# Scores of 64-wide heads: the queries' hi times the keys' lo on 128 rows, with a zero-padded block of queries, in place of 64 rows

## The chip, the cores and the metric

The kernel runs on one core of a Trainium2 chip. The metric is device time in microseconds (us), the median of three executions. One execution was also profiled; its trace is what the rows below come from. TensorE (PE) multiplies, VectorE (DVE) and ScalarE (ACT) work elementwise, GpSimd (POOL) does small elementwise work and issues some DMAs, and SyncE (SP) issues the weight loads. PEld is TensorE's loading of its stationary operand, which the profile lists beside the products.

## The reference

Two transformer blocks over 512 tokens of width 1024, in float32. Three places in them form scores between heads of width 64, and only these are touched by the change:

```
diff_attention:        sc = einsum('bqhcd,bkhcd->bchqk', q, k) * 64**-0.5      # 4 heads x 2, then softmax and a difference
chunk_band_attention:  sc = einsum('bqhd,bkhd->bhqk', q, k) * scale + bias     # 8 heads, softmax
dsa_attention:         s  = einsum('bqhd,bsd->bqhs', iq, ik) * idx_scale       # 16 index heads, one shared key
                       score = sum_h relu(s) * iw; sel = top_k(score, 128)
                       logits = q . k[sel] * 64**-0.5 + bias                   # 8 heads, softmax
```

Everything else (projections, up and down products, gates, a convolution, a recurrence) is large matrix products and elementwise work.

## The kernel before

Every operand of a product is split into two parts, hi and lo, whose sum is the float32 value; a product of two such operands is three products (hi·hi, hi·lo, lo·hi) that accumulate in one PSUM bank (`mm3`, lines 130 to 132, one "block" = three products of 128x512). Weights come as a stream of 512 KB loads, are split by ACT (L117) and DVE or POOL (L118), and feed generators of blocks.

For heads of 64 the kernel saves one of the three products. `pack_q` puts a head's 64 rows of hi and its 64 rows of lo above each other in one tile (`qhl`; for the odd head of a pair lo stands on top), `pack_k` makes a tile with the keys' hi twice (`khh`) and one with the lo of both heads of a pair (`kl`). `score` then makes two products into the same PSUM bank: L431, `qhl` against `khh` over all 128 rows (that is hi·hi + lo·hi), and L432, the head's own 64 rows of `qhl` against the same 64 rows of `kl` (hi·lo). The stationary operand is always 128 queries of one row tile i; the moving width is W = 128(i+1), since keys behind the row tile are not needed.

`score` is called in four stages. A: the first block's differential attention (tile `psa`, 4 heads x 4 row tiles = 16 steps of two scores, 32 in all), each score followed by a small bf16 product that masks a corner (L548, preceded by its own load of `identb`). B: the banded attention (`psc`, 16 steps, 32 scores, no mask product). I: the indexer (`psi`, 16 heads x row tiles 3, 2, 1 = 48 scores), where DVE sums the heads' relu (L899) and afterwards picks the 128 highest scores in 16 rounds per row tile (L908, L909); I call that stage S. D: the sparse attention (`psc` again, 32 scores, each followed by a bf16 mask product, L356).

A, B and D run as pipelines: a step is a generator, each `yield` is a round, and after each round the tracer puts some blocks of other products behind it (`self.fill(rate)`), which keep TensorE busy while DVE and ACT work on the softmax. The order of the instructions on each engine is fixed when the program is built. The bias tables of B and D (`bt`) are loaded by DMAs that POOL issues (L327), with a small memset on POOL behind each table in B (L329).

Of the kernel before, what the change touches and what calls it, by code (L numbers as in the profile page):

```python
# [8 lines left out]
F32 = mybir.dt.float32  # L9
F32R = mybir.dt.float32r  # L10
# [18 lines left out]
WBUFS = 2  # L29
RBUFS = 3  # L30
# [7 lines left out]
# the order of the banded attention's query (0) and key (1) tiles  # L38
# [25 lines left out]
def groups(n, head):  # L64
    """(first, length): a group of head, then ones"""
    return [(0, head)] + [(a, 1) for a in range(head, n)]


class Kern:
# [34 lines left out]
    def stream(self, src, eng=None):  # L104
        """yields (hi, lo) [128, 1024]: the next eight blocks; src [loads, 128, 1024]"""
# [21 lines left out]
    def mm3(self, out, w, x, start, stop):  # L127
        """w, x: (hi, lo) pairs; w stationary"""
        mm = self.nc.tensor.matmul
        mm(out, w[0], x[0], start=start, stop=False)  # L130
        mm(out, w[0], x[1], start=False, stop=False)  # L131
        return mm(out, w[1], x[0], start=False, stop=stop).ins  # L132

    # Products are generators: a step is one block. True: done a step; False: an operand
    # is not there yet.
    def fm(self, src, xs, evac, first=0, head=1, eng=None):
        """output tiles [128 features, tokens]: the first head tiles together, the contraction
        outermost, then one by one"""
# [16 lines left out]
    def tm512(self, src, xs, evac, eng=None):  # L155
        """token-major [tokens, 512 columns]: src [4, 128, 1024], rows of 512 over the contraction"""
# [21 lines left out]
    def lead(self, gen, n):  # L178
        """n blocks of gen; what the context traces for TensorE is queued behind them"""
# [4 lines left out]
    def fill(self, n):  # L184
        """traces up to n steps (a fraction carries over) of the products in line"""
# [12 lines left out]
    def finish(self, gen=None):  # L198
        """traces the line up to gen's end, or all of it"""
# [7 lines left out]
    def split(self, src, name, scale=None, n=T, tag="o", tag2=None):  # L207
        """(hi, lo) of src * scale, scale one value per partition"""
# [12 lines left out]
    def sumsq(self, xs, gain=None, n=T, sq_eng=None):  # L221
        """squares summed over the tiles"""
# [14 lines left out]
    def token_mean(self, acc, n=T, div=D, parts=P, eps=EPS):  # L237
        """summed over the partitions / div + eps, token-major [128, n/128]"""
# [10 lines left out]
    def norm(self, gen, acc):  # L249
        """1 / rms of the tokens, token-major and along the free axis, gen's first blocks between"""  # L250
# [11 lines left out]
    def diag(self, rs, n=T):  # L262
        """rs on the diagonals of [128, 128] blocks, as hi and lo"""
# [16 lines left out]
    def bcast(self, rs, n=T, dg=None):  # L280
        """[128, n] with rs[token] along the free axis on every partition"""
# [9 lines left out]
    def consts(self):  # L291
# [7 lines left out]
        self.corner = self.cp.tile([P, CUT], BF, name="corner")  # L299
        nc.sync.dma_start(self.vecs[:, :8], d["vecs"][:, :8])  # L300
# [5 lines left out]
        nc.vector.memset(self.corner[:CUT], NEG)  # L306

# [6 lines left out]
    def toeplitz(self, ext):  # L314
        """ext: two of [8, 384] -> loader of a head's table [128, 512]: row q is ext[255 - q:767 - q].
        Copies of ext one row apart in DRAM, read with a row step one short of a copy."""
# [17 lines left out]
    def bias_attention(self, qT, kT, v, load, masks, out, rate, packed=False):  # L334
        """qT, kT: 4 tiles of two heads, q scaled; v: token tiles [128, 512];
        masks: per query tile (mask [128, width] bf16, first column), or None when the
        table holds the mask; out: a list for 4 (hi, lo) feature tiles."""
# [3 lines left out]
        def step(p, i):  # L341
            W = P * (i + 1)
            if i == 0:
                st[p, "bt"] = [load(2 * p + a, masks is None) for a in range(2)]
            es, pts = [], []
            for a in range(2):
                h, r = 2 * p + a, slice(64 * a, 64 * a + 64)
                ps = self.ps.tile([P, T], F32, name="psc", tag="ps")
                if packed:
                    self.score(ps, qT[h], kT[h], 64 * a, i, W, masks is None)  # L350
# [40 lines left out]
    def pipeline(self, steps, rate, every=1):  # L391
        """traces the stages of successive steps, a step starting every so many rounds, and
        rate blocks of the products in line after each round"""
# [11 lines left out]
    # Scores of heads of 64 in float32 by two products: a head's (hi, lo) of the queries one above  # L405
    # the other against (hi, hi) of the keys, then hi against lo.
    def pack_q(self, z, tags):
        """z: two heads; -> a tile for each, hi in the head's rows and lo in the others"""
# [8 lines left out]
    def pack_k(self, z, tag):  # L417
        """z: two heads; -> for each (hi, hi), and the lo of both"""
# [9 lines left out]
    def score(self, ps, q, k, a, i, W, last=True):  # L428
        """ps: a row tile's scores of the head in rows a on of its tile"""
        w, r = q[:, i * P:i * P + P], slice(a, a + 64)  # L430
        self.nc.tensor.matmul(ps[:, :W], w, k[0][:, :W], start=True, stop=False)  # L431
        self.nc.tensor.matmul(ps[:, :W], w[r], k[1][r, :W], start=False, stop=last)  # L432

    def to_feature(self, o, name, scale=None, tag="y"):
        """four token blocks [128 tok, 4, 128 features] -> (hi, lo) feature tile"""
# [6 lines left out]
    def gelu2(self, u, t):  # L442
        """twice gelu of u (tanh form), into t"""
# [13 lines left out]
    def mix(self):  # L457
# [50 lines left out]
        # lambda  # L508
# [15 lines left out]
        # bias of the banded attention  # L524
# [13 lines left out]
        def step(h, i):  # L538
# [3 lines left out]
            r0 = st[h, "r0"]  # L542
            es, sm = [], self.small("sm2", 2)
            mx = self.small("mx2", 2)
            for c in range(2):
                ps = self.ps.tile([P, T], F32, name="psa", tag="ps")
                self.score(ps, qa[2 * h + c], ka[2 * h + c], 64 * c, i, W, False)
# [837 lines left out]
```

## Time and profile before

| what | value |
|---|---|
| median of three executions | 2321.76 us (2319.76 to 2322.29) |
| the profiled execution, span from first to last instruction | 2320.4 us; the page gives no other time for it |
| PE busy | 98% of the span |
| DVE busy | 60% |
| ACT busy | 39% |
| POOL busy | 10% |
| stage A | 94 to 187 us |
| stage B | 210 to 365 us |
| stage I | 989 to 1051 us |
| stage S | 1051 to 1131 us |
| stage D | 1119 to 1226 us |

The stages are read from the first and last instruction on their PSUM tiles. A busy PE is not a PE at its peak: the end of each product is modelled, so the length of a product on TensorE is read here from the start of one to the start of the next, and never from the listed duration.

### The profile page before, as it was taken

To read this page: it belongs to the slowest core of one execution; us is meant where nothing else is said; L and a number is where in the kernel's file an instruction comes from. 1 tells how busy PE (TensorE), PEld (TensorE's weight loads), DVE (VectorE), ACT (ScalarE), POOL (GpSimd) and SP (SyncE) were. 2 spreads that over 40 slices of the span, in tenths; PEclk is the share of its full clock that TensorE was granted. 3 is DMA by queue.
4 is the path that set the end of the run, shared out by engine and by line. 5 is a ranking of instruction groups with operands and counts; after the bars stand their busy time and mean duration, and the time that the engine had idled before them with its cause. 6 is when DMAs were issued, how large, how long until landed. Compare 5 with 4: busy or idle time off the path is not lost.

```text
span 2320.4 us, 28792 instructions
## 1 busy us (share of the span) xinstructions
PE 2268.6 (98%) x11254; PEld 1814.6 (78%) x11254; DVE 1391.8 (60%) x2391; ACT 914.8 (39%) x1426; POOL 235.6 (10%) x258
## 2 busy tenths in 40 slices
PE   7999999999999999998999999999999999999997
PEld 6777777888788888766667888888877778888886
DVE  7676555766443433579876777733465656777534
ACT  5454343544332222453463444422222234444322
POOL 3101100000111100113130000000111210000001
PEclk9999999999999999999999999999999999999999
DMA  4413323432533333322212333333321123333333
GB/s 141 98 55 92 91 64 100 146 91 73 101 97 100 95 97 100 94 61 78 73 46 86 96 95 97 100 95 99 91 64 56 56 64 91 100 95 97 100 93 107
DMA packets 62535, 207.27 MB, mean 89 GB/s; under 512 B 8216, under 2 KB 12384, under 8 KB 62400
## 3 DMA queue, kind: packets, MB, share of 16 engines
q1 hardware_dynamic: 58368, 198.60, 28.2%
q0 software_dynamic: 2880, 5.79, 1.7%
q8 instruction: 88, 1.44, 0.2%
q10 hardware_dynamic: 1152, 1.05, 0.1%
q14 instruction: 47, 0.39, 0.0%
HBM read 201.74 MB, written 3.67 MB: 89 GB/s over the span
## 4 chain that ended last, share of the span: by engine, by line
PE 91%; DVE 5%; ACT 1%; issue 1%; DMA 1%; POOL 1%; SPq 0%; DVEq 0%; ACTq 0%
PE pg L130 27%; PE pg L132 26%; PE pg L131 26%; PE pl L1112 1%; PE po L384 1%; PE ptr L372 1%; PE psc L432 1%; PE psi L432 1%; DVE wlo L118 1%; DVE isc L909 1%; PE psc L431 1%; DMA wraw<-in_w_in 1%; DVE m L908 1%; PE poh L1156 1%; PE poh L1155 0%
## 5 line engine op out<-in xcount | busy, mean ns | idle before, releaser
L117 ACT CAST whi<-wraw 128x1024 fp32r<-128x1024 f32 (+1 forms) x368 | 386.1, 1049 | 746.9 <-PE pg L131 472.3
L118 DVE TENSOR_TENSOR wlo<-wraw,whi 128x1024 fp32r<-128x1024 f32 (+1 forms) x356 | 436.4, 1226 | 314.6 <-ACT whi L117 308.9
L130 PE MATMUL pg<-fg2h,whi 128*128 128x512 f32 x704 | 274.1, 389 | 0.0
L132 PE MATMUL pg<-fg2h,wlo 128*128 128x512 f32 x704 | 273.9, 389 | 0.0
L131 PE MATMUL pg<-fg2l,whi 128*128 128x512 f32 x704 | 273.9, 389 | 0.0
L130 PEld LDWEIGHTS pg<-fg2h,whi 128*128 128x128 f32 x704 | 132.1, 188 | 27.6
L131 PEld LDWEIGHTS pg<-fg2l,whi 128*128 128x128 f32 x704 | 132.1, 188 | 27.5
L132 PEld LDWEIGHTS pg<-fg2h,wlo 128*128 128x128 f32 x704 | 132.1, 188 | 27.1
L132 PE MATMUL pg<-m2h,wlo 128*128 128x512 f32 (+1 forms) x374 | 140.9, 377 | 0.6 <-DVE wlo L118 0.6
L130 PE MATMUL pg<-m2h,whi 128*128 128x512 f32 (+1 forms) x374 | 141.0, 377 | 0.0
L131 PE MATMUL pg<-m2l,whi 128*128 128x512 f32 (+1 forms) x374 | 140.8, 377 | 0.0
L130 PE MATMUL pg<-fgh,whi 128*128 128x512 f32 x352 | 137.3, 390 | 0.9 <-ACT whi L117 0.9
L132 PE MATMUL pg<-fgh,wlo 128*128 128x512 f32 x352 | 137.1, 389 | 0.0
L131 PE MATMUL pg<-fgl,whi 128*128 128x512 f32 x352 | 137.0, 389 | 0.0
L1005 DVE SCALAR_TENSOR_TENSOR yc<-zc,vecs,yc 128x511 f32<-128x511 f32 (+1 forms) x176 | 130.8, 747 | 2.7
L130 PE MATMUL pg<-xgh,whi 128*128 128x512 f32 x256 | 105.3, 411 | 7.5 <-ACT xgh L216 6.4
L259 POOL TENSOR_TENSOR rs<-ms,mhalf 128x4 f32<-128x4 f32 (+1 forms) x11 | 12.9, 1175 | 945.3 <-DVE ms L246 591.4
L1001 DVE TENSOR_TENSOR zc<-pg,rsb 128x512 f32<-128x512 f32 x88 | 60.5, 688 | 74.1 <-PE pg L132 74.1
L131 PE MATMUL pg<-xgl,whi 128*128 128x512 f32 x256 | 101.7, 397 | 0.5 <-DVE xgl L217 0.5
L132 PE MATMUL pg<-xgh,wlo 128*128 128x512 f32 x256 | 102.0, 398 | 0.0
L132 PEld LDWEIGHTS pg<-m2h,wlo 128*128 128x128 f32 x374 | 70.4, 188 | 13.8 <-DVE wlo L118 0.8
L130 PEld LDWEIGHTS pg<-m2h,whi 128*128 128x128 f32 x374 | 70.3, 188 | 13.0
(422 smaller groups left out, 4790.1 us busy)
## 6 DMA issues: line engine op xcount, KB each, us to landing
wraw<-in_ffn_up SPq DMA_DIRECT2D x88, 512.0 KB, 3.5
wraw<-in_ffn_down SPq DMA_DIRECT2D x48, 512.0 KB, 3.5
wraw<-in_w_gate_up SPq DMA_DIRECT2D x44, 512.0 KB, 3.5
wraw<-in_w_in SPq DMA_DIRECT2D x39, 512.0 KB, 3.6
wraw<-in_c_in SPq DMA_DIRECT2D x32, 512.0 KB, 3.5
wraw<-in_ab SPq DMA_DIRECT2D x29, 512.0 KB, 3.6
wraw<-in_w_down SPq DMA_DIRECT2D x22, 512.0 KB, 3.6
wraw<-in_w_ckv SPq DMA_DIRECT2D x16, 512.0 KB, 3.6
```

Source lines behind the costliest of these rows:

```text
L117: nc.scalar.copy(hi[:, p], raw[:, p])
L118: eng.tensor_tensor(lo[:, p], raw[:, p], hi[:, p], op=ALU.subtract)
L130: mm(out, w[0], x[0], start=start, stop=False)
L131: mm(out, w[0], x[1], start=False, stop=False)
L132: return mm(out, w[1], x[0], start=False, stop=stop).ins
L372: nc.tensor.transpose(pt[:, j * P:j * P + P], es[a][:, j * P:j * P + P], self.ident)
L384: nc.tensor.matmul(po[r, i * P:i * P + P], v[j][:, c0:c0 + 64], pts[a][:, j * P:j * P + P], start=j == 0, stop=j == i)
L431: self.nc.tensor.matmul(ps[:, :W], w, k[0][:, :W], start=True, stop=False)
L432: self.nc.tensor.matmul(ps[:, :W], w[r], k[1][r, :W], start=False, stop=last)
L908: nc.vector.max(m8, a)
L1001: nc.vector.tensor_tensor(z, ps, rsb, op=ALU.mult)
L1005: nc.vector.scalar_tensor_tensor(y[:, sh:], z[:, :T - sh], self.col(f"cw{l}{j}", f), y[:, sh:], op0=ALU.mult, op1=ALU.add)
```

## The change

The second product of a score takes all 128 rows. In A, B and D a new helper `pad_q` copies the head's 64 rows of hi for the row tile into one of six tiles `zq` of 128x128 (three for heads whose hi stands on top, three for the others), whose other 64 rows were set to zero by six memsets on POOL at the start; the copy runs on POOL. The product is then `zq` against the whole `kl` tile. The copies of a step are issued in a round of their own, one `yield` ahead of its scores, so each pipeline is one round longer, and a copy waits until TensorE has read what stood in the tile three steps before. In I no copy is needed: both halves of the key's lo tile hold the same rows, and the second product takes `qhl` itself (so lo·lo is added as well). To make room for the six tiles, the scratch of POOL's DMA descriptors is halved to 8192 bytes per partition. The rest of the diff removes comments.

```diff
+ZBUFS = 3
...
+        self.zq, self.zn = [[self.cp.tile([P, P], F32R, name=f"zq{a}{n}") for n in range(ZBUFS)] for a in range(2)], 0
...
+        for z in self.zq[0] + self.zq[1]:
+            nc.gpsimd.memset(z.bitcast(F32), 0.0)
...
+            zs = [self.pad_q(qT[2 * p + a], 64 * a, i) for a in range(2)]
+            yield
...
-                    self.score(ps, qT[h], kT[h], 64 * a, i, W, masks is None)
+                    self.score(ps, qT[h], kT[h], zs[a], i, W, masks is None)
...
-    def score(self, ps, q, k, a, i, W, last=True):
-        w, r = q[:, i * P:i * P + P], slice(a, a + 64)
-        self.nc.tensor.matmul(ps[:, :W], w, k[0][:, :W], start=True, stop=False)
-        self.nc.tensor.matmul(ps[:, :W], w[r], k[1][r, :W], start=False, stop=last)
+    def pad_q(self, q, a, i):
+        z = self.zq[a // 64][self.zn % (2 * ZBUFS) // 2]
+        self.zn += 1
+        self.nc.gpsimd.tensor_copy(z[a:a + 64], q[a:a + 64, i * P:i * P + P])
+        return z
+    def score(self, ps, q, k, w, i, W, last=True):
+        q = q[:, i * P:i * P + P]
+        self.nc.tensor.matmul(ps[:, :W], q, k[0][:, :W], start=True, stop=False)
+        self.nc.tensor.matmul(ps[:, :W], q if w is None else w, k[1][:, :W], start=False, stop=last)
...
+            zs = [self.pad_q(qa[2 * h + c], 64 * c, i) for c in range(2)]
+            yield
...
-                self.score(ps, qa[2 * h + c], ka[2 * h + c], 64 * c, i, W, False)
+                self.score(ps, qa[2 * h + c], ka[2 * h + c], zs[c], i, W, False)
...
-            self.score(ps, iq[h], idx["k"], 64 * (h % 2), i, W)
+            self.score(ps, iq[h], idx["k"], None, i, W)
...
-    nc = _bacc.Bacc("TRN2", target_bir_lowering=False, num_devices=1)
+    nc = _bacc.Bacc("TRN2", target_bir_lowering=False, num_devices=1, dynamic_dma_scratch_size=8192)
```

On TensorE, the second step of stage A (row tile 1, W = 256), before and then after; `pta` are transposes, `pg` blocks of other products:

```order
L566 MATMUL pta<-ident,ea 128x128
L431 MATMUL psa<-khh,qhl 128x256
L432 MATMUL psa<-kl,qhl 128x256
L548 LDWEIGHTS identb
L548 MATMUL psa<-corner,identb 128x64
L431 MATMUL psa<-khh,qhl 128x256
L432 MATMUL psa<-kl,qhl 128x256
L548 LDWEIGHTS identb
L548 MATMUL psa<-corner,identb 128x64
```

```order
L582 MATMUL pta<-ident,ea 128x128
L445 MATMUL psa<-khh,qhl 128x256
L446 MATMUL psa<-kl,zq_100 128x256
L564 LDWEIGHTS identb
L564 MATMUL psa<-corner,identb 128x64
L445 MATMUL psa<-khh,qhl 128x256
L446 MATMUL psa<-kl,zq_103 128x256
L564 LDWEIGHTS identb
L564 MATMUL psa<-corner,identb 128x64
```

The products, their widths and their order are the same; the second one takes `zq`. In stage I not even a name changes.

On POOL, from the last head's norm of stage A (`rs`) into stage B, before and then after; `bt` are the bias tables, the L438 rows the new copies:

```order
L259 TENSOR_TENSOR rs<-hss,mhalf 128x4 x4
L327 DMA bt<-ext_dram 32x512 x5
L329 MEMSET bt 64x64
L327 DMA bt<-ext_dram 32x512 x7
L329 MEMSET bt 64x64 x2
L327 DMA bt<-ext_dram 32x512 x4
L329 MEMSET bt 64x64
L327 DMA bt<-ext_dram 32x512 x5
```

```order
L260 TENSOR_TENSOR rs<-hss,mhalf 128x4
L331 DMA bt<-ext_dram 32x512 x5
L333 MEMSET bt 64x64
L331 DMA bt<-ext_dram 32x512 x5
L333 MEMSET bt 64x64
L331 DMA bt<-ext_dram 32x512 x3
L333 MEMSET bt 64x64
L331 DMA bt<-ext_dram 32x512 x2
L438 COPY zq_100<-qhl 64x128
L331 DMA bt<-ext_dram 32x512
L438 COPY zq_103<-qhl 64x128
L333 MEMSET bt 64x64
```

The two copies that the first step of B needs (`zq_100`, `zq_103`) stand behind 15 and 16 DMA issues and three memsets; before, no instruction of TensorE waited for POOL there.

On TensorE, the end of stage B, from the last step's scores (W = 512) on, before and then after; `pg<-ob` are blocks of the product that follows, `po` and `ptr` the rest of the attention:

```order
L431 MATMUL psc<-khh,qhl 128x512
L432 MATMUL psc<-kl,qhl 128x512
L431 MATMUL psc<-khh,qhl 128x512
L432 MATMUL psc<-kl,qhl 128x512
L130 MATMUL pg<-obh,whi 128x512
L131 MATMUL pg<-obl,whi 128x512
L132 MATMUL pg<-obh,wlo 128x512
```

```order
L445 MATMUL psc<-khh,qhl 128x512
L446 MATMUL psc<-kl,zq_100 128x512
L445 MATMUL psc<-khh,qhl 128x512
L378 MATMUL ptr<-ident,sc 128x128
L390 MATMUL po<-pT,vb 64x128
L378 MATMUL ptr<-ident,sc 128x128
L390 MATMUL po<-pT,vb 64x128
```

Before, four blocks (twelve products) followed the last scores; after, they stand ahead of them.

## Rows read from the trace of the kernel before

**Rows 1.** The page: busy us of each engine, share of the span, instructions.

```profile
PE 2268.6 (98%) x11254; PEld 1814.6 (78%) x11254; DVE 1391.8 (60%) x2391; ACT 914.8 (39%) x1426; POOL 235.6 (10%) x258
```

**Rows 2.** Windows A, B, I, S, D: length, busy us of PE, PEld, DVE, ACT, POOL, clock, DMA.

```profile
94.00:200.00 106.00, 105.58 (x527) 82.64 (x526) 75.75 (x188) 53.79 (x121) 3.56 (x3) 1.00 0.21 65
200.00:365.00 165.00, 162.72 (x816) 122.65 (x816) 84.27 (x215) 67.28 (x139) 18.11 (x41) 1.00 0.28 84
...
989.00:1051.00 62.00, 62.00 (x213) 36.71 (x211) 47.67 (x71) 34.45 (x65) 7.46 (x5) 1.00 0.15 44
1051.00:1119.00 68.00, 59.55 (x249) 47.94 (x247) 64.64 (x145) 21.15 (x27) 22.58 (x12) 0.95 0.28 82
1119.00:1226.00 107.00, 105.14 (x612) 71.01 (x611) 78.97 (x239) 60.31 (x143) 25.17 (x29) 1.00 0.20 60
```

**Rows 3.** Timeline of PE: undisturbed runs of 128-row products, W = 512, then 256 (start, us).

```profile
119.78 0.39 PE L131 MATMUL pg<-wlo,xgh 128*128 128x512 f32 x1
...
122.04 0.39 PE L132 MATMUL pg<-whi,xgl 128*128 128x512 f32 x1
...
424.50 0.28 PE L131 MATMUL pg<-meml,whi 128*128 128x256 f32 x1
...
427.49 0.28 PE L132 MATMUL pg<-memh,wlo 128*128 128x256 f32 x1
```

**Rows 4.** Timeline of PE in stage I, scores of W = 512, 384 and 256.

```profile
1010.72 0.39 PE L431 MATMUL psi<-ikh,qhl 128*128 128x512 f32 x1
...
1011.80 0.40 PE L131 MATMUL pg<-egl,whi 128*128 128x512 f32 x1
1012.03 0.34 PE L431 MATMUL psi<-ikh,qhl 128*128 128x384 f32 x1
...
1013.64 0.40 PE L130 MATMUL pg<-egh,whi 128*128 128x512 f32 x1
```

**Rows 5.** Timeline of PEld beside it, idle before each load in brackets.

```profile
1011.04 0.18 PEld L432 LDWEIGHTS psi<-ikl,qhl 64*128 64x128 f32 x1 [0.36 <-issue]
1011.46 0.19 PEld L130 LDWEIGHTS pg<-egh,whi 128*128 128x128 f32 x1 [0.24 <-issue]
1011.57 0.19 PEld L131 LDWEIGHTS pg<-egl,whi 128*128 128x128 f32 x1
```

**Rows 6.** Timeline of PE in stage B: a step of W = 512, one of 128.

```profile
351.75 0.47 PE L431 MATMUL psc<-khh,qhl 128*128 128x512 f32 x1
...
353.78 0.40 PE L131 MATMUL pg<-obl,whi 128*128 128x512 f32 x1
...
246.34 0.30 PE L431 MATMUL psc<-khh,qhl 128*128 128x128 f32 x1
...
247.67 0.39 PE L131 MATMUL pg<-xgl,whi 128*128 128x512 f32 x1
```

**Rows 7.** Timeline of PE in stage A: a step of W = 512 with its corner products.

```profile
110.78 0.48 PE L431 MATMUL psa<-khh,qhl 128*128 128x512 f32 x1
...
112.49 0.20 PE L548 MATMUL psa<-corner,identb 128*128 128x64 bf16 x1
112.53 0.48 PE L130 MATMUL pg<-whi,xgh 128*128 128x512 f32 x1
112.85 0.39 PE L131 MATMUL pg<-wlo,xgh 128*128 128x512 f32 x1
```

**Rows 8.** Timeline of POOL between stages A and B.

```profile
202.23 1.01 POOL L259 TENSOR_TENSOR rs<-hss,mhalf 128x4 f32<-128x4 f32 x1 [23.62 <-DVE hss L636]
...
211.54 1.96 POOL L327 DMA_DIRECT2D bt<-ext_dram  x4 [0.29 <-issue]
```

**Rows 9.** Groups on POOL, shapes apart: busy us, mean ns of one, idle before.

```profile
L1098 POOL TENSOR_TENSOR dt<-dt 128x64 f32<-128x64 f32 x8 | 3.1, 386 | 0.6
```

**Rows 10.** Timeline of DVE in stage S: one form with POOL at work, and without.

```profile
1054.40 2.30 DVE L413 TENSOR_TENSOR qhl<-zq,qhl 64x512 fp32r<-64x512 f32 x1
...
1057.19 0.69 DVE L413 TENSOR_TENSOR qhl<-zq,qhl 64x512 fp32r<-64x512 f32 x1
```

## The prediction

> **What bounds the kernel now.** I read the page's busy times first: TensorE is busy for 98% of the span and no other engine for more than 60% [rows 1]. So whatever shortens TensorE's own work shortens the kernel, except where another engine is nearly as full. The windows tell where that is [rows 2]: in A, B and D, TensorE is busy 105.6 of 106, 162.7 of 165 and 105.1 of 107 us, with DVE at 71%, 51% and 74%. In I it is busy all 62 us, but DVE already has 47.7. In S the roles are exchanged: DVE 64.6 of 68, TensorE 59.6. The granted clock is 1.00, that is 2.4 GHz, in all but S.
>
> A busy TensorE hides waste, so next I read the steps from start to start. Ten products of 128 rows and W = 512 take 122.04 - 119.78 = 2.26 us, 0.226 each; 25 of W = 256 take 2.99 us, 0.12 each [rows 3]. For W = 384 I take the middle, 0.173 (an estimate). That is the price of a product whose neighbours are of its own kind. Round a 64-row product it is different [rows 4, 5]. L431 starts at 1010.72, and the load for L432 only at 1011.04: 0.32 later instead of 0.226, and PEld stood idle for 0.36 before it, waiting for nothing that the profile shows. L432's successor begins its load at 1011.46, 0.42 later; that one, too, was not loaded ahead (PEld idle 0.24), and its own successor's load comes 0.11 behind, when the stream begins. So on both sides of the 64-row product the array runs empty (about 0.1 us) and a load (about 0.1 us) lies open. That is some 0.4 us per score, none of it shown as idle TensorE.
>
> **What the change gives on TensorE.** The new second product has 128 rows like its neighbours, so I price it as theirs. I take each stretch from the first L431 to the second start behind its scores.
>
> In I: the score of 512 with the next product, 1010.72 to 1011.80, is 1.08 us for three products; at 0.226 they are 0.68: 0.40 less. The scores of 384 and 256 with the next product, 1012.03 to 1013.64, are 1.61 us; 2 x 0.173 + 2 x 0.12 + 0.226 = 0.81: 0.80 less [rows 3, 4]. That is 1.20 per index head, and 16 x 1.20 = 19.2 us.
>
> In B: a step (two scores) of 512 takes 351.75 to 353.78 = 2.03; five products at 0.226 and 0.09 for the first load, which the short transposes ahead don't cover, are 1.22: 0.81 less. The 0.09 is what the product behind a short one takes over 0.226: 112.53 to 112.85 [rows 7]. For W = 384 and 256 I take I's 0.80. For W = 128 a stream is shorter than a load, so the load's 0.11 [rows 5] is the step: 246.34 to 247.67 = 1.33 against 4 x 0.11 + 0.226 + 0.09 = 0.76: 0.57 less [rows 6]. Four steps: 2.98; four pairs of heads: 11.9 us.
>
> In A: the corner product is so short that the load behind it stays open with either version. The step of 512 takes 110.78 to 112.85 = 2.07; after: 5 x 0.226, three open loads of 0.09 and two corners of 0.04 (112.49 to 112.53) are 1.48: 0.59 less, 0.22 under B's [rows 7]. With that for all widths, four steps give 2.98 - 0.88 = 2.10, four heads 8.4 us. D has the same steps with a mask product instead: 8.4 us.
>
> Together 47.9 us of TensorE's time. The lower bound for each score is nothing at all (a rival below); W = 128 at half a load would add 2 us and no more.
>
> **What of it reaches the end.** A: nothing else there is over 71%, and the blocks that run between the steps last beyond the stage: 8 of the 8.4, the rest for softmax results that now have a shorter cover; bounds 5 and 8.4.
>
> B: two subtractions. The copies of its first step stand behind 15 and 16 of POOL's DMA issues; in the trace the sixteen end 211.54 + 1.96 - 202.23 = 11.3 us after `rs` starts [rows 8], and stage B's first score came at 210, some 8 us after it, now with four blocks (2.7 us) more ahead: TensorE waits 0 to 3 us, I take 0.5. At the end the last scores lose the four blocks behind them, 12 x 0.226 = 2.7 us of cover; 2.3 us of idle stand in that stage already [rows 2], because cover was short before, so I take 1.5 of the 2.7. 11.9 - 2 = 9.9; bounds 6 and 11.9.
>
> I and S: TensorE's 62 us would become 43, but DVE needs 47.7 in that window [rows 2]. In S, where it is the bound, DVE is 95% full; at that density 47.7 us take 50, so the window can shrink by 12, by 14 if DVE never stood still. Scores come in threes and DVE's other work (queries' lo, the first block's norm) is not spread evenly: I take 10, bounds 4 and 14. S itself stays as long as DVE's rounds, and TensorE idles there more than now.
>
> D: DVE at 79 of 107 would be at 80% of 98; its start overlaps the last selection. I take 6 of 8.4, bounds 2 and 8.4.
>
> The copies: 64 on POOL (32 steps, two each). The trace has no copy of this form; the nearest row is a two-input product of 128x64 at 386 ns [rows 9], a copy of 64x128 has one input. I take 0.3 us, between 0 and 0.4: 19 us on an engine that is busy 10%. They are issued a round ahead, over 3 us before their product, so I cost them at nothing on the path; that cover is gone where POOL is blocked, which is B's start, above. While POOL computes, a DVE instruction can stretch: L413 took 2.30 us instead of 0.69 [rows 10]. At up to 0.4 us each, six copies ahead of S and 26 in D are at most 2.4 us where DVE is the bound, inside I's bounds. The six memsets at the start run while POOL waits for the first input. The smaller DMA scratch I cost at nothing: the tables of 64 KB are spread over the stages, and their wait is already priced.
>
> The Trainium skill, "SBUF — State Buffer", section "SBUF: two separate sides", says that a POOL instruction holds a port pair for its whole length against DVE instructions with two SBUF inputs; by it, 32 copies of 0.4 in S and D would cost DVE 13 us, 2.4 of them in S, and the sum would be 2290 instead of 2288. L413's 2.30 agrees with it.
>
> Sum: 8 + 9.9 + 10 + 6 = 33.9 us. From the span, 2320.4 - 33.9 = 2286.5; the median stands 1.4 above the span, so **2288 us** (1.5% less). With all lower bounds 17 us, with all upper ones 42.7.
>
> **Rivals.** (1) *Other engines eat most of it.* DVE's 51% to 74% are averages; if I gives 4 and the shorter rounds leave softmax results late in A, B and D, less than the lower bounds remains: a gain of 5 to 17 us, about 2310. For it: S and the idle 2.3 us in B. Against it: there is almost no idle on TensorE in A, B and D, so covers have room today.
>
> (2) *The 64 rows are not the cause.* If the emptying came from the second product itself (same bank, a new stationary operand), it would stay, and the pipelines would only get their longer tail: 2321.8 + 2 = 2324. Against it: L130 to L132 also write one bank with changing operands, at 0.226.
>
> (3) *The second product waits for its copy, step after step.* TensorE takes its instructions in order, so a late copy holds the masks, transposes and blocks behind it. A copy needs the tile that was read three steps before, and POOL in order. Break-even is at 33.9 / 32 = 1.06 us per step; if each pair stood behind four table issues (1.96 us, rows 8) beyond its cover, 32 x 1.96 = 63 us are lost: 2288 + 63 = 2351. Against it: steps are over 5 us apart and POOL is busy 18 of 165 us in B and 25 of 107 in D.
>
> (4) *Padding gives up work that ran side by side.* If L432 shared the array with its neighbour today, the full array would cost its stream: at 0.173 for the mean width, 144 x 0.173 = 25 us, 2347. Against it: the successor's load starts 0.42 us after L432's, later than behind any full product [rows 5]. The Trainium skill, "TensorEngine Tiling (Array Packing)", section "Theoretical Speedup", promises up to twice the rate for 64 rows, and so speaks against this change; the trace differs, since here the neighbours take all 128 rows.
>
> **How the numbers follow.** The forecast with its bounds (gain 17 to 43) has 0.68, rival 1 0.19, rival 2 0.05, rival 3 0.06, rival 4 0.02. Leaving out rivals 2 to 4 and the outer half of rival 1, the range is 2275 to 2311. About 0.2%, or 4.6 us, is what a measurement of this kernel can tell from no change. Faster: 0.68 + 0.19 = 0.87; within: rival 2, 0.05; slower: rivals 3 and 4, 0.08.
>
> **What the profile after would show.** L431 to the second product 0.226 at W = 512 and 0.12 at 256, and no "issue" idle on PEld there: the price is right. TensorE's busy time down by some 40 us, and more idle than 8.4 us in S: DVE is the bound there. DVE over 85% in I. POOL's copies near 0.3 us. Wrong would be: 64-row steps unchanged (rival 2); idle on TensorE whose releaser is the copy's line (rival 3); idle behind DVE's softmax lines in A, B or D (rival 1).

## The result

The changed kernel takes **2289.2 us** (median of 4 runs, 2288.6 to 2292.4), the kernel before 2321.2 beside it: ratio 0.9866, 95% interval 0.9854 to 0.9878. Forecast were 2288, with a range of 2275 to 2311. The profiled execution took 2289.7 us, its span 2287.9 instead of 2320.4. The lines of the code have moved: L431 and L432 are now L445 and L446, L130 to L132 are L131 to L133.

The page's busy times, against [rows 1]:

```profile
PE 2226.7 (97%) x11254; PEld 1808.5 (79%) x11254; DVE 1390.4 (61%) x2391; ACT 912.3 (40%) x1426; POOL 272.0 (12%) x360
```

TensorE has lost 41.9 us of busy time, and the span is 32.5 us shorter, so TensorE is idle for 9.4 us more (61.2 instead of 51.8, span less busy). DVE and ACT do what they did; POOL has 36.4 us more. The same five stages, against [rows 2] (length, then busy us of PE, PEld, DVE, ACT, POOL, the granted clock, the DMA's share):

```profile
94.00:198.00 104.00, 100.96 (x541) 82.32 (x540) 75.53 (x190) 53.99 (x122) 16.13 (x36) 1.00 0.26 70
198.00:346.00 148.00, 146.33 (x794) 116.68 (x794) 80.54 (x212) 65.15 (x137) 25.50 (x67) 1.00 0.30 89
972.00:1024.00 52.00, 48.13 (x211) 36.32 (x210) 46.38 (x69) 32.69 (x65) 10.81 (x9) 0.97 0.18 52
1024.00:1092.00 68.00, 60.74 (x252) 49.23 (x252) 65.36 (x147) 21.88 (x29) 22.87 (x14) 0.92 0.27 82
1092.00:1194.00 102.00, 96.71 (x606) 69.74 (x606) 82.22 (x239) 59.25 (x143) 33.95 (x55) 0.98 0.21 63
```

I's window (third line) is 10 us shorter, and DVE is busy for 89% of it instead of 77%; S is as long as it was. TensorE now idles 3 us in A and 5 in D, where there were 0.4 and 1.9.

Where the time went is read from five marks that both traces have:

| from the start of the span to | before | after | gained up to here |
|---|---|---|---|
| first product of the first block's `w_out` (behind B) | 378.5 | 361.0 | 17.5 (A and B) |
| first index score | 989.0 | 971.6 | 17.4 |
| first selection (DVE's MAX8) | 1051.7 | 1025.5 | 26.2 (I: 8.8) |
| last selection | 1140.0 | 1114.1 | 25.9 (S: -0.3) |
| first product of the second gated feed-forward | 1265.4 | 1232.8 | 32.6 (D: 6.7) |

From there to the end nothing changes (1055 us in both).

The step itself, in I (timeline of PE, start and duration in us), against [rows 4]:

```profile
987.04 0.39 PE L445 MATMUL psi<-ikh,qhl 128*128 128x512 f32 x1
987.26 0.39 PE L446 MATMUL psi<-ikl,qhl 128*128 128x512 f32 x1
987.49 0.33 PE L445 MATMUL psi<-ikh,qhl 128*128 128x384 f32 x1
987.66 0.34 PE L446 MATMUL psi<-ikl,qhl 128*128 128x384 f32 x1
987.84 0.40 PE L131 MATMUL pg<-egh,whi 128*128 128x512 f32 x1
988.07 0.39 PE L132 MATMUL pg<-egl,whi 128*128 128x512 f32 x1
```

and PEld beside it, against [rows 5]:

```profile
987.04 0.19 PEld L446 LDWEIGHTS psi<-ikl,qhl 128*128 128x128 f32 x1
987.27 0.19 PEld L445 LDWEIGHTS psi<-ikh,qhl 128*128 128x128 f32 x1
987.49 0.19 PEld L446 LDWEIGHTS psi<-ikl,qhl 128*128 128x128 f32 x1
987.66 0.19 PEld L131 LDWEIGHTS pg<-egh,whi 128*128 128x128 f32 x1
```

Product follows product at 0.22 to 0.23 (W = 512) and 0.17 to 0.18 (384), where a 64-row product's neighbours stood 0.32 and 0.42 off. Each load starts with the product ahead of it; the idle that stood in brackets in [rows 5] is gone. In A, the second score of a step of 512 with its corner product and the next block, against [rows 7]:

```profile
112.16 0.47 PE L445 MATMUL psa<-khh,qhl 128*128 128x512 f32 x1
112.48 0.40 PE L446 MATMUL psa<-kl,zq 128*128 128x512 f32 x1
112.72 0.21 PE L564 MATMUL psa<-corner,identb 128*128 128x64 bf16 x1
112.76 0.47 PE L131 MATMUL pg<-whi,xgh 128*128 128x512 f32 x1
113.07 0.39 PE L132 MATMUL pg<-wlo,xgh 128*128 128x512 f32 x1
```

That is 0.91 us, of which the load behind a corner product still lies open twice (0.32 and 0.31 instead of 0.23). The forecast's prices give 3 x 0.226 + 2 x 0.09 + 0.04 = 0.90.

### The profile page after: what moved, and what is told of

Its sections match the earlier page's. It is cut to its first block, busy times and chain, and to the rows that moved or that the text cites. A ratio compares the mean times of both kernels' runs of the same rounds, so it can differ in the third digit from the quotient of the medians.

```text
span 2287.9 us, 28921 instructions
## 1 busy us (share of the span) xinstructions
PE 2226.7 (97%) x11254; PEld 1808.5 (79%) x11254; DVE 1390.4 (61%) x2391; ACT 912.3 (40%) x1426; POOL 272.0 (12%) x360
## 4 chain that ended last, share of the span: by engine, by line
PE 86%; DVE 9%; ACT 2%; issue 1%; POOL 1%; DMA 0%; SPq 0%; DVEq 0%; ACTq 0%; POOLq 0%
PE pg L131 26%; PE pg L132 25%; PE pg L133 25%; PE pl L1128 1%; DVE isc L925 1%; DVE wlo L119 1%; PE po L390 1%; DVE m L924 1%; PE ptr L378 1%; ACT whi L118 1%; DVE qhl L419 1%; DVE khh L429 1%; DVE isc L915 1%; PE poh L1172 1%; PE poh L1171 1%
## 5 line engine op out<-in xcount | busy, mean ns | idle before, releaser
L131 PE MATMUL pg<-fg2h,whi 128*128 128x512 f32 x704 | 274.1, 389 | 0.0
L133 PE MATMUL pg<-fg2h,wlo 128*128 128x512 f32 x704 | 273.9, 389 | 0.0
L132 PE MATMUL pg<-fg2l,whi 128*128 128x512 f32 x704 | 273.9, 389 | 0.0
L131 PEld LDWEIGHTS pg<-fg2h,whi 128*128 128x128 f32 x704 | 132.2, 188 | 27.4
L133 PEld LDWEIGHTS pg<-fg2h,wlo 128*128 128x128 f32 x704 | 132.2, 188 | 27.4
L132 PEld LDWEIGHTS pg<-fg2l,whi 128*128 128x128 f32 x704 | 132.2, 188 | 27.4
L133 PE MATMUL pg<-m2h,wlo 128*128 128x512 f32 (+1 forms) x374 | 140.9, 377 | 0.6 <-DVE wlo L119 0.6
L131 PE MATMUL pg<-m2h,whi 128*128 128x512 f32 (+1 forms) x374 | 141.0, 377 | 0.0
L132 PE MATMUL pg<-m2l,whi 128*128 128x512 f32 (+1 forms) x374 | 140.8, 376 | 0.0
L131 PE MATMUL pg<-fgh,whi 128*128 128x512 f32 x352 | 137.3, 390 | 0.9 <-ACT whi L118 0.9
L133 PE MATMUL pg<-fgh,wlo 128*128 128x512 f32 x352 | 137.1, 389 | 0.0
L132 PE MATMUL pg<-fgl,whi 128*128 128x512 f32 x352 | 137.0, 389 | 0.0
L131 PE MATMUL pg<-xgh,whi 128*128 128x512 f32 x256 | 103.9, 406 | 7.1 <-ACT xgh L217 5.9
L132 PE MATMUL pg<-xgl,whi 128*128 128x512 f32 x256 | 101.9, 398 | 0.5 <-DVE xgl L218 0.5
L133 PE MATMUL pg<-xgh,wlo 128*128 128x512 f32 x256 | 101.2, 395 | 0.0
L133 PEld LDWEIGHTS pg<-m2h,wlo 128*128 128x128 f32 x374 | 70.3, 188 | 13.6 <-DVE wlo L119 0.8
L131 PEld LDWEIGHTS pg<-m2h,whi 128*128 128x128 f32 x374 | 70.3, 188 | 13.0
```

## Experiments

Ratios are those to the kernel before, measured beside each run, with 95% intervals; its median lay between 2320.7 and 2321.3.

| run | what it is | us | ratio |
|---|---|---|---|
| e1_index_only | 128 rows in I alone | 2311.1 | 0.9957 (0.9943 to 0.9970) |
| e2_abd_only | 128 rows in A, B, D alone | 2298.2 | 0.9902 (0.9888 to 0.9915) |
| e3_copies_64rows | all the additions, 64 rows | 2321.5 | 1.0003 (0.9994 to 1.0012) |
| e4_no_copies | 128 rows everywhere, no additions | 2288.3 | 0.9858 (0.9844 to 0.9871) |
| e5_twice | 64-row product issued twice | 2352.0 | one run |
| e6_no_norm | e4, eight DVE instructions left out of I | 2284.7 | 0.9843 (0.9827 to 0.9860) |
| e7_a_round | e4, one more round in A | 2287.9 | 0.9857 (0.9843 to 0.9872) |
| e8_norm_off_dve | e4, the eight instructions on ACT and POOL | 2287.6 | 0.9857 (0.9842 to 0.9872) |
| e9_one_block | the changed kernel, one padded block, no extra round | 2288.0 | 0.9859 (0.9842 to 0.9875) |

### One stage at a time

e1, against the kernel before:

```diff
-            self.score(ps, iq[h], idx["k"], 64 * (h % 2), i, W)
+            self.score(ps, iq[h], idx["k"], 64 * (h % 2), i, W, full=True)
...
+        r = slice(0, P) if full else r
         self.nc.tensor.matmul(ps[:, :W], w[r], k[1][r, :W], start=False, stop=last)
```

> Only the indexer's 48 scores (stage I) take their second product on 128 rows; the 96 scores of A, B and D stay on 64 rows, there are no copies, no extra round, and the DMA scratch is as before. Theory (each 64-row product costs TensorE emptying and an open load, and DVE limits what of it I can use): I shortens as it did in the changed kernel, 8 to 10 us, and nothing else moves: 2311 to 2313 us. The 48 scores' own starts then fall from 31.9 us (before) to about 19.4 (after). Rival: the gain between the first index score and the last selection came from the copies' and rounds' other timing, or is handed back in S and D: 0 to 3 us, 2318 to 2321. Rival: the whole of TensorE's 12.6 us counts: 2309.

e2, against the changed kernel:

```diff
-        self.nc.tensor.matmul(ps[:, :W], q if w is None else w, k[1][:, :W], start=False, stop=last)
+        r = slice(0, P)
+        if isinstance(w, int):
+            r, w = slice(w, w + 64), q
+        self.nc.tensor.matmul(ps[:, :W], w[r], k[1][r, :W], start=False, stop=last)
...
-            self.score(ps, iq[h], idx["k"], None, i, W)
+            self.score(ps, iq[h], idx["k"], 64 * (h % 2), i, W)
```

> The changed kernel with the indexer's second product back on 64 rows: copies, padded blocks, the extra round and the smaller DMA scratch stay, and A, B and D run on 128 rows. Theory: A and B together keep their 17.5 us, S and D their 6.4, I is as long as before (61 us from its first score to its last): 2297 us. If D's gain hung on I's, less: 2300 to 2303. Together with the run in which only I is changed, the two gains should add up to the 32.5 us of the changed kernel within 2 us; if they add up to less, the stages share a bound (DVE in S and the start of D).

e1 came out at 2311.1, inside the theory's 2311 to 2313, and e2 at 2298.2, 1 us over its 2297. e1 gained 9.55 us, e2 22.48, together 32.0: what the changed kernel gains (32.0). The stages do not share a bound that the sum would show. In e2, I is as long as before, 61.2 us (970.8 to 1032.0, first to last index score); in e1 it has fallen to 51.9 (987.2 to 1039.0).

### The price of the additions

e3, against the changed kernel: the copied block is used, but only the head's 64 rows of it.

```diff
...
-        self.nc.tensor.matmul(ps[:, :W], q if w is None else w, k[1][:, :W], start=False, stop=last)
+        r = slice(a, a + 64)
+        self.nc.tensor.matmul(ps[:, :W], (q if w is None else w)[r], k[1][r, :W], start=False, stop=last)
...
```

> The changed kernel, but every second product uses 64 rows again: in A, B and D the head's 64 rows of the copied block, in I those of its own tile. So the 96 copies, TensorE's dependence on them, the extra round and the smaller DMA scratch are there, and the 128 rows are not. It measures the price of all that the change adds. Theory (copies hidden, a round ahead of their product): 0 to 3 us over before, 2320 to 2324, with the scores' starts as far apart as before (0.41 to 0.43 us for 512 columns in B). The forecast's third rival in a mild form (a step now and then waits for its copy, or DVE is held by POOL): 0.1 us in each of 48 steps or more, 2326 and above, with TensorE idle before the second product and the copies' line as releaser. If the copies or the extra round help, below 2319.

e4, against the kernel before:

```diff
-        self.nc.tensor.matmul(ps[:, :W], w[r], k[1][r, :W], start=False, stop=last)
+        self.nc.tensor.matmul(ps[:, :W], w, k[1][:, :W], start=False, stop=last)
```

> 128 rows in all four stages without any copy: the second product takes the queries' packed tile itself (hi in the head's 64 rows, lo in the other 64) against the lo of both heads' keys, so in A, B and D it adds a term that the reference doesn't have, the lo of one head's queries times the lo of the other head's keys. No padded blocks, no extra round, DMA scratch as before. Theory (the gain is the rows; the copies lie hidden): 2286 to 2290 us, the same as the changed kernel within 3 us; TensorE's steps in A, B and D equal to the changed kernel's. If the copies cost something (DVE stretched by POOL, the extra round in the pipeline), it is below the changed kernel by what the kernel with copies on 64 rows lies over before. If the gain hung on the padded block (another stationary tile in the second product, so that its load can run ahead), the steps are as long as before: about 2311.

Copies, extra round, memsets and the smaller scratch cost 0.8 us of 2321, inside the interval of no change; the 128 rows alone give the whole gain. Busy times of e3, then of e4:

```profile
PE 2265.6 (98%) x11254; PEld 1811.9 (78%) x11254; DVE 1392.7 (60%) x2391; ACT 914.6 (39%) x1426; POOL 273.2 (12%) x360
```

```profile
PE 2226.8 (97%) x11254; PEld 1808.3 (79%) x11254; DVE 1390.3 (61%) x2391; ACT 913.5 (40%) x1426; POOL 235.3 (10%) x258
```

TensorE's 2226.8 us in e4 are the changed kernel's 2226.7: whether the second product's block is a padded copy or the queries' own tile makes no difference to TensorE. DVE is at 1390.4 with the copies and 1390.3 without.

e9, against the changed kernel:

```diff
-ZBUFS = 3
+ZBUFS = 1
...
             zs = [self.pad_q(qT[2 * p + a], 64 * a, i) for a in range(2)]
-            yield
```

(and the same `yield` in A).

> The changed kernel with one padded block for each half of the rows instead of three, and without the extra round: a copy can only start when TensorE has read the same block for the step before, and it is issued in the round of its product. Theory (steps lie 4 to 10 us apart, and a copy needs 0.3 us on an engine that is 12% busy, so it is done long before its product; the three blocks and the round buy nothing): as the changed kernel, 2287 to 2291 us, no idle of TensorE whose releaser is the copy's line. Rival (the forecast's third: copies that wait for TensorE's last read hold POOL's queue, with the tables' DMAs behind them, and the next product waits for its copy): 0.3 us or more in each of the 48 steps, 2303 us or more, with the copy's line as releaser of idle TensorE.

2288.0: the theory's. Even a copy that can start only when the step before has been read comes in time. The tiles named `zq` in the changed kernel (copies with their shortest, median and longest ns, and what POOL was idle for ahead of them, in us and times):

```profile
L438 POOL CAST zq<-qhl x96: 282/292/1006, 42.1 to 1164.0; 64x128 fp32r<-64x128 f32 x96
...
  PE psa L564: 88.1, 21
  PE psc L446: 84.5, 25
```

It is POOL that waits for TensorE, not the other way. In the traces of the changed kernel and of e9, TensorE's only wait for POOL is that for the weights' `wlo`, 1.8 us, once; none names the copies' line.

### Is it the 64-row product, or the change to it and back?

e5, against the kernel before:

```diff
+        self.nc.tensor.matmul(ps[:, :W], w[r], k[1][r, :W], start=False, stop=False)
         self.nc.tensor.matmul(ps[:, :W], w[r], k[1][r, :W], start=False, stop=last)
```

> The kernel before with the 64-row product issued twice in a row in all 144 scores (its term enters the scores twice). Theory (what costs is the change between 128 and 64 rows, on both sides): the first product is as far from the first 64-row product as before (0.33 to 0.41 us for 512 columns), the second 64-row product as far from its successor as before (0.42), and between the two 64-row products lies only a stream: 0.23 us for 512 columns, 0.18 for 384, 0.12 for 256. Rival (every 64-row product is dear by itself, whatever stands beside it): 0.42 between the two, 0.37 and 0.31 for 384 and 256. In time: 144 x 0.16 = 23 us over before for the first, 144 x 0.35 = 50 us for the second, less what DVE doesn't let through.

One score of 512 (L433 is the second 64-row product) on PE and on PEld, where the bracket is the idle time ahead:

```profile
1009.23 0.39 PE L431 MATMUL psi<-ikh,qhl 128*128 128x512 f32 x1
1009.55 0.50 PE L432 MATMUL psi<-ikl,qhl 64*128 64x512 f32 x1
1009.89 0.39 PE L433 MATMUL psi<-ikl,qhl 64*128 64x512 f32 x1
1010.21 0.45 PE L431 MATMUL psi<-ikh,qhl 128*128 128x384 f32 x1
```

```profile
1009.55 0.18 PEld L432 LDWEIGHTS psi<-ikl,qhl 64*128 64x128 f32 x1 [0.35 <-issue]
1009.66 0.19 PEld L433 LDWEIGHTS psi<-ikl,qhl 64*128 64x128 f32 x1
1010.21 0.19 PEld L431 LDWEIGHTS psi<-ikh,qhl 128*128 128x128 f32 x1 [0.36 <-issue]
```

From L431 to its successor of 128 rows it is 0.98 us; before, with one 64-row product, 0.32 + 0.42 = 0.74. The second 64-row product has added 0.24, one stream. The load of L433 starts 0.11 behind that of L432, with no idle and well ahead of its product; the two loads at a change of height start only when their product does, 0.35 and 0.36 us of idle behind the load ahead. So one 64-row product or two cost the same 0.3 us over the streams (0.74 - 2 x 0.226 and 0.98 - 3 x 0.226): the change costs, not the height. Both 64-row products here take the same rows and the same operand; two with different operands in a row were not run. In its details the expectation missed: 0.34 lie between the two 64-row products and 0.32 behind them, not 0.23 and 0.42. The sum is that of the theory, and 0.1 us of it shows one product earlier.

In time, the 144 added products cost 30.7 us, more than the 23 of the theory, less than the 50 of the rival. The starts account for 24; TensorE's busy time rose by 27.1 and its idle by 2.7. Most of the 3 us between starts and busy time goes with the clock: in e5's trace TensorE was busy for 24.3 us at a granted clock of 0.50, before for 18.8, and at half the clock half of the 5.5 us more is time added, 2.7 us (an estimate).

### What holds I now

e6, against e4:

```diff
-            elif h > 3 and h % 2 == 0:
-                for f in {4: (0,), 6: (1,), 8: (2, 3), 10: (4, 5), 12: (6,), 14: (7,)}[h]:
-                    t = self.u("x2", "x")
-                    nc.vector.scalar_tensor_tensor(t, xs[f], self.col("norm_final_g", f), r1b,
-                                                   op0=ALU.mult, op1=ALU.mult)
-                    xs[f] = t
```

> The kernel with 128 rows and no copies, with the eight DVE instructions in stage I left out that apply the first block's final norm (they run there in two groups of four, 5.3 and 3.1 us; the norm is missing from what follows). They take 8.2 us of DVE's time in I. Theory (in I it is DVE that eats a part of TensorE's gain: TensorE idles 4.1 us there behind ACT's reads of the score tiles, which wait for DVE, and its clock falls to half after the longest of these waits): the idle goes, I shortens by 4 to 6 us, and the kernel stands at 2282 to 2284 us. Rival (the score tiles and ACT's own pace hold TensorE): the idle stays, 2287 to 2289. Rival (what I gains, S gives back, since DVE is full there): first selection earlier by 4 to 6 us, but the end less than 1 us earlier; against it, S has no instruction that waits for I's end.

e8, against e4:

```diff
-                    nc.vector.scalar_tensor_tensor(t, xs[f], self.col("norm_final_g", f), r1b,
-                                                   op0=ALU.mult, op1=ALU.mult)
+                    nc.scalar.activation(t, xs[f], AF.Identity, scale=self.col("norm_final_g", f))
+                    nc.gpsimd.tensor_tensor(t, t, r1b, op=ALU.mult)
```

> The kernel with 128 rows and no copies, with the same eight instructions moved off DVE: ACT scales by the weight, POOL multiplies by the tokens' factor (8 of each). Theory (DVE limits I): 2283 to 2286, a little above the version that leaves the norm out, since ACT has to do 8 x 0.5 us in a stage where it is at about half, and POOL's two-input products can stretch DVE's two-input instructions. Rival: that stretching costs as much as was taken off DVE (POOL is busy 8 x 1 us or more, DVE waits that long): 2288 or more.

The changed kernel first. Timelines of DVE, ACT and PE in the middle of I:

```profile
983.78 2.07 DVE L915 SCALAR_TENSOR_TENSOR isc<-irel,iw,isc 128x256 f32<-128x256 f32 x4
985.77 5.33 DVE L940 SCALAR_TENSOR_TENSOR x<-x,vecs,rsb 128x512 f32<-128x512 f32 x4
991.13 0.69 DVE L419 TENSOR_TENSOR qhl<-pg,qhl 64x512 fp32r<-64x512 f32 x1
```

```profile
991.85 0.58 ACT L418 CAST qhl<-pg 64x512 fp32r<-64x512 f32 x1 [2.44 <-DVE qhl L419]
992.45 0.87 ACT L908 ACTIVATE irel<-psi 128x256 f32<-128x256 f32 x2
```

```profile
990.35 0.40 PE L132 MATMUL pg<-egl,whi 128*128 128x512 f32 x1
992.89 0.44 PE L445 MATMUL psi<-ikh,qhl 128*128 128x384 f32 x1 [2.14 <-ACT irel L908]
...
994.40 0.63 PE L131 MATMUL pg<-egh,whi 128*128 128x512 f32 x1
...
996.88 0.39 PE L131 MATMUL pg<-egh,whi 128*128 128x512 f32 x1
```

Four norms stand in a row on DVE, until 991.1. Behind them comes DVE's part of the queries' split (L419, until 991.82); ACT's cast for the next part (L418) waits 2.44 us for that, ACT's reads of the score tiles (L908) stand behind the cast, and TensorE waits 2.14 us for one. In e6, without the norms, this wait is gone, and the kernel is 3.6 us faster than e4 (2284.1 to 2285.3 against 2287.2 to 2289.1), less than the 4 to 6 of the theory. I (first to last index score) falls from 50.6 to 47.9, and S from 88.2 to 86.9; S lies between 86.8 (e9) and 93.1 us (e5) in the other traces, though no run changed its work, so this second fall proves nothing. The granted clock is 1.00 in all of I in e4, so what the expectation says of the clock holds for the changed kernel's trace and not for the one that e6 is set against. Five short waits of TensorE for the same read stay, 1.7 us in all, with DVE busy 43.0 of 52 us: part of the idle was not the norms' doing. Nothing was given back in S.

In e8 DVE has nothing of the norms either, and nothing measurable was gained: 2287.6, between the theory's 2286 and the rival's 2288. Timelines of POOL and DVE:

```profile
981.59 12.11 POOL L925 TENSOR_TENSOR x<-x,rsb 128x512 f32<-128x512 f32 x8 [12.40 <-DVE isc L899]
```

```profile
982.35 5.51 DVE L899 SCALAR_TENSOR_TENSOR isc<-irel,iw,isc 128x256 f32<-128x256 f32 x4
...
1002.22 2.07 DVE L899 SCALAR_TENSOR_TENSOR isc<-irel,iw,isc 128x256 f32<-128x256 f32 x4
```

While POOL multiplied, four accumulations took 5.51 us; when it was idle, 2.07. On the page DVE is busy for 1391.6 us, against 1390.3 in e4, although eight instructions of 8.2 us are gone. That is the rival's reason: what was taken off DVE came back as stretching. I lasted 52.7 us instead of 50.6, but not all of that is DVE's: behind a wait of 2.57 us the granted clock fell to 0.50 in e8's I, and in e4's it did not.

### More cover in A

e7, against e4:

```diff
             nc.vector.scalar_tensor_tensor(at[:, :W], es[1][:, :W], cf, es[0][:, :W], op0=ALU.mult, op1=ALU.add)
             yield
+            yield
```

> The kernel with 128 rows and no copies, with one more round (5.7 blocks of the projections) in stage A between a step's scores and its transposes. Theory (the shorter steps took from the softmax's cover, which cost A 2.3 us of idle behind DVE there): the idle goes and the time falls by 1 to 2.3 us, to 2286 to 2287.5. Rival (the longer pipeline makes its tail dearer, or the tiles that are held for one more round run out): no change or up to 2 us more, 2288 to 2290.

No change: the waits in A are still 2.3 us, behind another instruction. PE's waits in stage A, of e4 and then of e7 (us in all, times, longest):

```profile
PE pta L566 <- DVE ea L562: 2.3, 4, 1.1
```

```profile
PE pta L567 <- DVE yal L217: 2.3, 2, 1.5
```

With the longer pipeline the softmax result (`ea`) is ready, but the transposes now stand behind DVE's split of a finished head (`yal`). The rival was right about the time; its reasons (the tail, tiles that run out) do not show.

Of e4, e6, e7, e8 and e9 only e6, which leaves work out, can be told from the changed kernel by its time. e4 and e9 give the same time with less.

## Why the forecast held, and where its steps did not

**The price of a 64-row product** was right in kind. It was set at some 0.4 us per score, worked out by stage. From the starts of all scores in both traces, with the product behind each where it is a block of the projections, listed idle left out:

| stage | forecast, TensorE | measured | forecast, reaching the end | measured |
|---|---|---|---|---|
| A | 8.4 | 8.6 | 8 | together 17.5 |
| B | 11.9 | 11.7 | 9.9 | |
| I | 19.2 | 15.6 | 10 | 8.8 |
| S | 0 | 0 | 0 | -0.3 |
| D | 8.4 | 8.1 | 6 | 6.7 |
| sum | 47.9 | 44.0 | 33.9 | 32.5, with 0.2 of rounding and places between the marks |

TensorE's busy time on the page fell by 41.9, less than these 44.0. The clock can account for the rest: TensorE was busy for 24.9 us at a granted clock of 0.50 in the changed kernel's trace, for 18.8 before, and at half the clock half of the 6.1 us more, 3 us (an estimate), is time added, most of it outside the scores.

The mis-sized term is **I, 1.20 us per index head**, where 0.97 came. The time before was right: 2.71 us per head on average, 2.69 by [rows 4]. The time after was 1.74, not 1.49, since the forecast priced every product as undisturbed. In 18 of the 48 scores the load of the first product could not begin until ACT had read the score tile (`irel`). Timelines of PEld and PE for such a score of W = 256 in the changed kernel:

```profile
1009.36 0.19 PEld L445 LDWEIGHTS psi<-ikh,qhl 128*128 128x128 f32 x1 [0.27 <-ACT irel L908]
1009.47 0.19 PEld L446 LDWEIGHTS psi<-ikl,qhl 128*128 128x128 f32 x1
```

```profile
1009.36 0.39 PE L445 MATMUL psi<-ikh,qhl 128*128 128x256 f32 x1
1009.58 0.28 PE L446 MATMUL psi<-ikl,qhl 128*128 128x256 f32 x1
```

The load starts with its product instead of ahead of it, and the second product comes 0.22 behind, not 0.12. So it is in 11 of the 16 scores of W = 256, in 3 of W = 384 and in 4 of W = 512, each some 0.1 us longer than the undisturbed ones: 2 of the 3.6 us that are missing. In these 18 the product ahead is longer, too (0.32 instead of 0.23), and none of it is listed as idle TensorE. Before, the two products of W = 256 stood 0.22 apart as well, but in 15 of 16 cases without such a wait: that was the change to 64 rows. The forecast's next bound, which it priced apart from the step, is thus in part inside the step.

**What of it reaches the end.** Two terms were off and nearly cancelled; that A and B together came within 0.4 us of the forecast's 17.9 is luck. B lost nothing of the 2 us taken off: no wait for the first step's copies shows behind the tables' DMAs, and the tail waits 1.7 us for ACT's transposes (`pT`), 1.6 before. A lost more: it waits 2.9 us for the softmax, 0.4 before, where 0.4 were taken off. That its steps have become shorter than DVE's work on them is the likely reason; e7 gave this work more cover and the wait went, but another took its place. In I the forecast's mechanism (DVE is the next bound) holds in part: 3.9 us of idle, up from none; of the 4.1 that e4 has in their place, e6 removed 2.4. About 1 us more went to the clock (last section). DVE's density came out at 89% in the window, not the 95% of S from which the 10 us were derived. S stayed as long, and D gave 6.7 for 6. One sign missed: in S TensorE should have idled more than its 8.4 us, and it idles 7.3 (68 - 60.74, in the windows above).

**The copies** cost nothing, as forecast, but their number was wrong: 48 steps (16 each in A, B and D) with two each make 96, not 64 in 32 steps. The error had no part in the sum, since their cover was priced at nothing, but it stood in two places: POOL's 19 us were 36.4 (with the six memsets), and the break-even of the third rival was 33.9 / 48 = 0.71 us per step, not 1.06. The estimate of 0.3 us, under the 386 ns of [rows 9], was right at the median (0.29); the longest took 1.0.

The Trainium skill, "SBUF — State Buffer", section "SBUF: two separate sides", calls the port pair of POOL and DVE an exclusive lock for a whole instruction, and by it the forecast gave 2290. The copies, which read one operand, took no more than 1 us from DVE in either pair of runs (1390.4 against 1390.3, 1392.7 against 1391.8), not 13. Where one met a two-operand DVE instruction under way, it was the copy that grew: 0.83 us at 143.18 in the changed kernel, beside an L419 that kept its 0.69. For POOL's products of two operands e8 shows what the page says, in 5.51 against 2.07 us.

**The rivals.** (1) happened in part: 11.5 of 44.0 us did not reach the end, but it needed 27 or more for a gain of at most 17. (2) fell with the step in I above, against [rows 4], and with e4. (3) fell with e3 and e9. (4) fell with the result, and with e5: beside a 64-row product nothing ran side by side, it stopped the load behind it. The Trainium skill, "TensorEngine Tiling (Array Packing)", has under "Key Properties" a sentence that bears on this: "Changing tiling mode (not just tile) drains the TensorE". e5 agrees: the load is late at 128 to 64 and at 64 to 128, and not between 64 and 64. There and back it costs 0.3 us here.

## What to carry over

In this kernel a product on half the rows between products on all rows is not cheaper but dearer, by 0.3 us: compare starts, not busy times, since the busy engine hides it. If a pad of zeros costs a copy on an idle engine and a step's worth of time ahead, fill the rows; if the other half's rows hold something harmless, as in e4, not even the copy is needed. Count the gain by stage, and take off what the next engine needs there, also where its waits hide inside a step.

## What the runs showed of the chip beyond that

After TensorE's 2.14 us of idle in I, its products of 512 columns followed each other at 0.43 us instead of 0.23 for a while, with no idle between. The windows ahead, in and behind (us, busy us of PE and the others, then the granted clock):

```profile
989.00:992.80 3.80, 1.75 (x8) 1.12 (x7) 3.74 (x4) 1.34 (x5) 1.55 (x1) 1.00 0.32 72
993.50:996.50 3.00, 3.00 (x9) 2.45 (x9) 2.97 (x6) 0.87 (x2) 0.00 (x0) 0.50 0.05 19
997.00:1000.00 3.00, 3.00 (x16) 2.52 (x15) 1.91 (x3) 1.10 (x2) 0.00 (x0) 1.00 0.00 0
```

The granted clock is 0.50 there, 1.2 GHz, and 1.00, 2.4 GHz, on both sides. The six steps from 994.40 to 996.88 took 2.48 us for 1.36, 1.1 us more. The stage before the change had no such wait and ran at 1.00 throughout.

The wait alone does not decide it. In e4 the same wait stands in the same place, and the clock stayed at 1.00 in all of I (timeline of PE, then the window):

```profile
990.85 0.44 PE L431 MATMUL psi<-ikh,qhl 128*128 128x384 f32 x1 [2.14 <-ACT irel L892]
```

```profile
970.00:1022.00 52.00, 47.88 (x216) 36.09 (x216) 47.83 (x71) 32.75 (x65) 7.85 (x5) 1.00 0.18 52
```

e1 and e9 have the wait and the fall, like the changed kernel, and their I lasts 51.9 us like its own; e4 and e7 have the wait without the fall, and theirs lasts 50.6 and 50.9. So the fall costs about 1 us here, and what decides whether it comes is open. An engine that is relieved and then waits can so lose a part of its gain to its clock.
